# A hybrid RWKV-7 block on one core: other rules for the planner's buffers, four column tiles at the beginning, and a smaller margin

## The chip, the cores and the metric

The kernel runs on one core of a Trainium2 chip. The metric is the device time of one execution in microseconds (us); lower is better. An engine in this text is one of TensorE (PE in the profile; PEld is its weight load), VectorE (DVE), ScalarE (ACT), GpSimd (POOL) and SyncE (SP), which issues the transfers.

## The reference

One layer works on a residual stream x of 1024 positions by 1024 channels, all in float32. Cut to what matters:

```python
h = rms_norm(x, norm_mix)
p = h @ W_in        # columns: r,k,v (512 each) | decay 64 | a 64 | gate 160 | conv b,c,x (512 each) | gates a,b (1024 each)
y_a = rwkv7_branch(...)     # S_t = S_{t-1} diag(w_t) + (S_{t-1} a_t) b_t^T + v_t k_t^T;  y_t = S_t r_t, 8 heads of 64
y_b = B * conv3(C * x_c)
x += (sigmoid(gA) * (y_a @ P_A) + sigmoid(gB) * (y_b @ P_B)) @ W_o
x += cross_attention(rms_norm(x), rms_norm(mem))   # 4 heads of 256, 256 memory tokens: K, V = mem @ w_kv
x += relu(rms_norm(x) @ W_up) ** 2 @ W_down        # 4096 wide
return rms_norm(x)
```

## The kernel before

Channels lie on the partitions and positions in the free dimension, in two blocks of 512 positions (block 0 and 1). A product of the full precision is made in three: each operand is held as a high part in a short float format and the remainder as a low part, and high by high, high by low and low by high are summed in a PSUM bank. So one column tile (128 output channels) over one block is 8 k-tiles of 3 matmuls of 512 columns: 24.

A weight goes through four stages. SP loads it raw (tag `wr`, two buffers), ScalarE makes the high part (`wh`), VectorE subtracts it from the raw one to make the low part (`wl`), TensorE multiplies. `w_loads` (L428) starts load i when the weights before i - 2 are split, and `w_splits` (L515) lets only a few split weights wait for TensorE.

**The order of the work** is not found by the chip. A planner (`Scheduler`, L46 to L243) runs while the program is built: every part of the kernel is a generator that yields the time or condition at which its next step makes sense; `run` takes the streams on the side in turn when they are ready and else the main stream, and every instruction is written to its engine's queue in the order in which it is recorded. The planner's clock is the estimated end of TensorE's queue. `cost` estimates an instruction, `need(t)` is the estimated end of the writes to t plus 0.7 us, `pace(engine)` the end of an engine's queue less 0.3 us. All instructions come from one helper line (L256 in the profile), so groups in the profile are told apart by the tiles. An engine executes its queue in order: where TensorE's next matmul waits, everything behind it waits.

PSUM has 8 banks, in tags: `g` three (projections; `psg` in the profile), `s` two (`pss`), `c` two (`psc`), `y` one (`psy`). Which buffer a new tile of a tag gets is decided by the framework underneath when the program is built. `slot` (L296) is the planner's model of that choice: of the buffers in use, it takes the one whose estimated end is earliest, and counts the new tile as writable from then.

**The beginning.** x arrives in eight row pieces, four for each block. `x_stage(b)` (L1026) transposes them on TensorE in two halves of channels, into banks of `s` and `c`, scales them by the norm's gain, and splits them into high and low (tiles `H`). `gemm` with pair=2 (L826) starts the projection with two column tiles at once: block 0 for both, then block 1 for both; then one column tile after another. `constants` (L707) transposes the small parameter vectors and derives constants on GpSimd.

**The RWKV part** is cut into 8 windows (4 pairs of heads by 2 blocks). `wkv_prepare` (L1274) makes a window's operands; its small matrix products go through the two banks of tag `s` (norms, the four products of `evac_products`, two groups of transposes, bonus, values, and more in `wkv_invert` and `wkv_out`: 13 tiles in each window). They are made as side streams while the projection's large products run. `take_s` and `give_s` count the banks of `s` in use, and a product is recorded when its inputs are `need` + `LATE` old, where `LATE` is 0.7 (L1258).

**The end of the projections.** While the last windows' chains run, the projection of the gates (2 x 8 column tiles) and the memory's keys (`mem_k`, 8 tiles) and values (`mem_v`, 2 x 4 weights) fill TensorE. `HEAD` (L607) is the number of projection tiles that run before the memory's; the last four (`ga` 4 to 7) stand between them: keys 0 to 3, gate tile 4, keys 4 to 7, gate tile 5, first half of the values, gate tile 6, second half, gate tile 7. A weight of the keys or values has half as many product columns as a gate's (`light`).

Then follow the merge of the two branches, the output projection, the attention and the MLP.

Of the kernel before, what the change touches and what calls it, by code (L numbers as in the profile page):

```python
# [41 lines left out]
class Scheduler:  # L42
# [4 lines left out]
    def __init__(self, nc):  # L47
        self.nc = nc
        self.free = {"PE": 0.0, "DVE": 0.0, "ACT": 0.0, "POOL": 0.0, "SP": 0.0, "DMA": 0.0, "LD": 0.0}
        self.writes, self.reads, self.base, self.end = {}, {}, {}, {}  # L50
        self.side = []
        self.cold = 10
        self.mode = (128, 128)
        self.port = {"DVE": [], "POOL": []}
# [13 lines left out]
    def cost(self, eng, meth, aps):  # L68
# [3 lines left out]
        if eng == "ACT":  # L72
            return (0.05 if psum else 0.093) + (0.093 if len(aps) > 2 else 0.0) + n / 1200 + (0.1 if part and n > 64 else 0.0)
        if eng == "DVE":
# [4 lines left out]
            if part:  # L79
                return (0.2 if meth == "scalar_tensor_tensor" else 0.17) + (0.08 if 4 < n <= 64 else 0.0) + n * 0.00104  # L80
            if meth in ("tensor_scalar", "tensor_copy") and not psum:
                return 0.12 + n * 0.00068
# [75 lines left out]
    def note(self, eng, meth, outs, ins):  # L158
# [25 lines left out]
        for a in outs:  # L184
            k, r = self.key(a), self.region(a)
            self.writes[k] = [x for x in self.writes.get(k, ()) if x[1] > old and x[0] != r] + [(r, end, lat, eng)]
            self.end[k] = max(self.end.get(k, 0.0), end)

# [73 lines left out]
def tile_hybrid_block(  # L262
# [31 lines left out]
    slots = {}  # L294

    def slot(tag, t):  # L296
# [113 lines left out]
    def w_raw(i):  # L410
        n = 2 if i in quads else 1
        more = i >= first_quad and (i - first_quad) % 2 if i in quads else i > first_quad and i % 4 > 1
# [15 lines left out]
    def w_loads():  # L428
        for i in range(2, len(wlist)):
# [85 lines left out]
    def w_splits():  # L515
        for i in range(2, len(wlist)):
# [20 lines left out]
            yield lambda: ws["made"] < ws["closed"] + (4 if i < 4 else 2 if i < first_quad else 3)  # L537
# [69 lines left out]
    HEAD = len(PROJ) - 4  # L607
    wcols = [w_cols(win, job_off(k, i), n=32 if (k, i) == ("gd", 1) else P) for k, i in PROJ]
    wlist += wcols[:HEAD]
    for q in range(2):  # L610
        i = len(wlist)
        wlist += [w_cols(w_kv[0], n * P) for n in range(4 * q, 4 * q + 4)]
        light.update(range(i, len(wlist)))
        wlist.append(wcols[HEAD + q])
    for n in range(2):
        i = len(wlist)
        wlist += [w_wide(w_kv[0], kq * 256, D + n * 512) for kq in range(4)]
        light.update(range(i, len(wlist)))
        wlist += wcols[HEAD + 2 + n:HEAD + 3 + n]
# [27 lines left out]
    for i in range(2):  # L647
        w_load_half(i, SP, 1)
    for i in range(4, 8):
# [57 lines left out]
    def constants():  # L707
        yield until(("h", 0, 3))
        yield need(vrow) + 6.0
        vps = ps("g", [P, P])  # L710
# [4 lines left out]
        yield until(("r1", 0))  # L715
# [110 lines left out]
    def gemm(jobs, xh, xl, evac, key=None, scale=None, pair=1):  # L826

        def finish(t, b, o):
            if scale is not None:
                yield until((scale, b))  # L830
            yield room
            evac(t, b, o)

        group = pair
        while jobs:
            now, jobs = jobs[:group], jobs[group:]
            ws_ = []
            for t in now:
                yield from w_take(ws_)
            for b in range(NB):  # L840
                os_ = [ps(t, [P, TB]) for t in (("g", "y") if group == 2 and b else ("g", "g"))[:group]]
                yield need(*os_)
                for k in range(KD):
                    if key is not None:
                        yield until((key, b, k))
                    for (wh, wl), o in zip(ws_, os_):
                        if wl is None:
                            yield need(wh, xl[k][b])
                            mm(o[:], wh[:, k, :], xh[k][b], k == 0, False)
                            yield  # L850
                            mm(o[:], wh[:, k, :], xl[k][b], False, k == KD - 1)
                            yield
                            continue
                        yield need(wl[:, k], xl[k][b])
                        yield from mm3y(o[:], wh[:, k, :], wl[:, k, :], xh[k][b], xl[k][b], k == 0, k == KD - 1)
                if b == NB - 1:
                    for _ in now:
                        w_close()
                for t, o in zip(now, os_):
                    yield from finish(t, b, o)  # L860
            group, key = 1, None
# [151 lines left out]
    def x_scale(b, xs, ss):  # L1013
        cs = slice(0 if b else TB, D)
        junk = sb("P", [P, D]) if b else None
        for i in range(4):
            ACT.activation(junk[:] if b else xs[i][:, cs], xs[i][:, cs], AF.Square, accum_out=ss[:, 4 + i:5 + i])
# [5 lines left out]
        yield from over_partitions(r, Rt[:, b], "g", 4.0 * b)  # L1023
        done.add(("r1", b))

    def x_stage(b, tags):  # L1026
# [3 lines left out]
        if b:  # L1030
            yield until(("h", 0, KD - 1))
        else:
            w_first()
        for h in range(2):
            o = [ps(t, [P, TB]) for t in tags[h]]
            for i in range(4):
                yield need(xs[i][:, h * TB:(h + 1) * TB], *o)
# [82 lines left out]
    def lora_side(name, parts, b, dst, fin):  # L1120
        yield until(("x", 1))
        for j in range(4):
# [11 lines left out]
            fin(z, o2, j)  # L1134
            dma(dst[cs, blk(b)], z, (name, j, b))
# [122 lines left out]
    LATE = 0.7  # L1258
# [6 lines left out]
    def give_s():  # L1265
# [8 lines left out]
    def wkv_prepare(w):  # L1274
# [67 lines left out]
        give_s()  # L1342
# [9 lines left out]
        def evac_products(o, q, h):  # L1352
# [10 lines left out]
            give_s()  # L1363
# [18 lines left out]
        for q in range(2):  # L1382
# [5 lines left out]
            give_s()  # L1388
            ACT.activation(BKt[:, 4 * q:4 * q + 4].rearrange("p c h k -> p c (h k)"), o[:], AF.Copy)
        w["BKt"] = BKt  # L1390
        yield until(("val", j, b))

    def bonus_and_values(w, rk_, vs_, ta_, tm_):
# [20 lines left out]
        give_s()  # L1414
# [15 lines left out]
        give_s()  # L1430
# [14 lines left out]
    def wkv_invert(w):  # L1445
# [46 lines left out]
        give_s()  # L1492
# [10 lines left out]
        give_s()  # L1503

    def wkv_chain(ws):
# [20 lines left out]
        def finish(c):  # L1526
# [3 lines left out]
            if c % 2:  # L1530
                for i, w in enumerate(ws):
                    ACT.activation(flat(w)[:, (c - 1) * C:(c + 1) * C],
                                   Y[c // 2][:, i].rearrange("p a n -> p (a n)"), AF.Copy)

        for c in range(NCH):
# [38 lines left out]
            for q in range(2):  # L1574
# [6 lines left out]
                for h, H, i, w in PART[q]:  # L1581
# [3 lines left out]
                    else:  # L1585
                        DVE.tensor_scalar(new, o2[q][H, 2, i % 2], pc, None, op0=ALU.mult)
            if last:
# [649 lines left out]
```

## Time and profile before

| | us |
|---|---|
| median of 3 runs (lowest, highest) | 1776.28 (1775.63, 1779.83) |
| the profiled execution, its span | 1777.75, 1776.0 |
| TensorE busy | 1726.2 (97%) |
| VectorE, ScalarE, GpSimd busy | 1079.9, 693.2, 520.4 |
| mean granted clock of TensorE | 0.989 |

A row of the page's list of groups or of a timeline names line, engine, operation, output <- inputs, and the shape; in a timeline the start and the length stand ahead, and in brackets how long the engine was idle before it and what released it. A row of the table by stages has the stretch, its length, the busy time of each engine with its instructions, TensorE's granted clock (1.00 is full), the share of the DMA engines' time, and GB/s.

### The profile page before, as it was taken

How to read it: one execution, taken by the hardware profiler on the slowest of the kernel's cores; microseconds unless marked ns; L12 is line 12 of the kernel's file. 1: busy time of each engine (PE TensorE's matmuls, PEld its weight loads, DVE VectorE, ACT ScalarE, POOL GpSimd, SP SyncE). 2: the span in 40 equal slices, each digit the busy share in tenths (PEclk: the TensorE clock that was granted, in tenths of full speed). 3: DMA queues.
4: the chain of work that ended last, by engine and by line, in shares of the span. 5: the costliest groups of instructions: out<-in, count | busy, mean ns of one | idle time of the engine just before them, and what ended most of it. 6: DMA issues, size and time to landing. Idle time of an engine off the chain costs nothing. (4 is left out here: it accounts for less than half of the span.)

```text
span 1776.0 us, 26498 instructions
## 1 busy us (share of the span) xinstructions
PE 1726.2 (97%) x9818; PEld 1421.6 (80%) x9818; DVE 1079.9 (61%) x1700; ACT 693.2 (39%) x1256; POOL 520.4 (29%) x879
## 2 busy tenths in 40 slices
PE   7999999989999999999999999999999999999998
PEld 5787778778778787788888888878888888888887
DVE  4577684556763545565557665596776775555543
ACT  6624221332313563322323434454444453534532
POOL 3136658218286003001313335343323310000000
PEclk9999999999999998999999999999999999999999
DMA  6733533314543428645645667345454489655441
GB/s 215 252 120 99 154 87 86 85 40 133 158 113 117 120 84 273 213 143 202 225 148 166 204 208 253 101 136 179 148 184 149 137 272 351 247 190 190 154 131 48
DMA packets 299007, 289.18 MB, mean 163 GB/s; under 512 B 40488, under 2 KB 217758, under 8 KB 298878
## 3 DMA queue, kind: packets, MB, share of 16 engines
q1 hardware_dynamic: 297806, 286.97, 50.2%
q8 instruction: 77, 1.26, 0.3%
q10 hardware_dynamic: 1072, 0.53, 0.1%
q14 instruction: 52, 0.43, 0.1%
HBM read 193.06 MB, written 94.37 MB: 162 GB/s over the span
## 5 line engine op out<-in xcount | busy, mean ns | idle before, releaser
L256 PE MATMUL psg<-H,wh 128*128 128x512 f32 x1808 | 582.6, 401 | 4.9 <-ACT wh L256 3.5
L256 PEld LDWEIGHTS psg<-H,wh 128*128 128x128 f32 x1808 | 342.1, 191 | 77.4 <-ACT wh L256 4.4
L256 PE MATMUL psg<-P,wh 128*128 128x512 f32 (+1 forms) x1240 | 371.6, 380 | 0.8 <-DVE P L256 0.8
L256 PE MATMUL psg<-H,wl 128*128 128x512 f32 x888 | 354.7, 399 | 0.1
L256 PEld LDWEIGHTS psg<-P,wh 128*128 128x128 f32 x1240 | 228.3, 188 | 44.0 <-DVE P L256 1.2
L256 ACT ACTIVATE wh<-wr 128x1024 fp32r<-128x1024 f32 (+2 forms) x180 | 137.0, 787 | 296.0 <-PE psg L256 200.7
L256 PE MATMUL psg<-P,wl 128*128 128x512 f32 (+1 forms) x620 | 235.5, 380 | 0.0
L256 DVE TENSOR_TENSOR wl<-wr,wh 128x1024 fp32r<-128x1024 f32 (+2 forms) x171 | 166.7, 994 | 60.6 <-ACT wh L256 57.9
L256 PEld LDWEIGHTS psg<-H,wl 128*128 128x128 f32 x888 | 169.8, 191 | 35.9 <-DVE wl L256 0.9
L256 ACT ACTIVATE P<-P 128x512 fp32r<-128x512 f32 (+2 forms) x258 | 153.6, 630 | 81.5 <-DVE P L256 49.9
L256 DVE TENSOR_TENSOR P<-P,P 128x512 fp32r<-128x512 f32 (+2 forms) x221 | 155.8, 740 | 20.7 <-ACT P L256 19.2
L256 POOL TENSOR_TENSOR sm<-sm,mhalf 128x8 f32<-128x8 f32 (+3 forms) x19 | 23.3, 1232 | 464.8 <-DVE sm L256 464.8
L256 PEld LDWEIGHTS psg<-P,wl 128*128 128x128 f32 x620 | 116.6, 188 | 21.4
L256 POOL TENSOR_TENSOR ex<-ex,P 128x60 f32<-128x60 f32 (+24 forms) x248 | 95.9, 387 | 37.2 <-DMA P<-dn 21.3
L256 PE MATMUL pss<-P,wh 128*128 128x512 f32 x304 | 94.5, 390 | 1.6 <-DVE P L256 1.6
L256 POOL TENSOR_TENSOR ex<-ex 128x60 f32<-128x60 f32 (+24 forms) x248 | 90.0, 363 | 19.4
L256 DVE TENSOR_TENSOR P<-psg,P 128x512 f32<-128x512 f32 x44 | 30.3, 688 | 82.6 <-PE psg L256 68.8
L256 DVE TENSOR_TENSOR st<-psg,P 128x512 f32<-128x512 f32 x40 | 27.6, 691 | 75.6 <-PE psg L256 70.5
L256 PEld LDWEIGHTS pss<-P,wh 128*128 128x128 f32 x304 | 57.1, 188 | 14.8 <-DVE P L256 2.9
L256 PE MATMUL psc<-P,wh 128*128 128x512 f32 x216 | 66.5, 389 | 0.0
L256 ACT ACTIVATE P<-P,vec 128x512 f32<-128x512 f32 (+2 forms) x57 | 40.5, 711 | 65.6 <-DVE P L256 54.8
L256 DVE TENSOR_SCALAR P<-psc,sm 64x64 f32<-64x64 f32 x120 | 32.3, 290 | 53.8 <-ACT P L256 53.7
(684 smaller groups left out, 2772.5 us busy)
## 6 DMA issues: line engine op xcount, KB each, us to landing
P<-d_t SPq DMA_DIRECT2D x56, 512.0 KB
wr<-in_w_in_dram SPq DMA_DIRECT2D x40, 512.0 KB
d_t<-P SPq DMA_DIRECT2D x64, 256.0 KB
d_x<-P SPq DMA_DIRECT2D x48, 256.0 KB
P<-d_x SPq DMA_DIRECT2D x24, 512.0 KB
d_t<-st SPq DMA_DIRECT2D x48, 256.0 KB
d_tg<-st SPq DMA_DIRECT2D x32, 256.0 KB
wr<-in_w_kv_dram SPq DMA_DIRECT2D x16, 512.0 KB
```

The source lines that it names most:

```text
L256: return fn(*args, **kw)
```

## The change

The instructions are the same on every engine to within a few; what changes is their order up to the merge. In its parts:

- **The model of the buffers.** The planner counts instructions and keeps, for each tile, the number of its last use. `slot` takes the buffer with the earliest last use, and of those first one that was handed back by a call of `free` (`give_s(o)` does that now with the bank it gives back).
- **Costs.** An activation on less than 128 partitions costs 0.1 us more whatever its length, a scan has its own cost.
- **The beginning.** `gemm_first` does the first four column tiles: 0 and 1 over block 0, 2 and 3 over block 0, then 0 and 1, and 2 and 3 over block 1. The raw weights 2 and 3 are loaded by SP ahead of the second four pieces of x. The transposes of block 1 wait for the parameter vectors ("vec"), which are handed over with 2.0 us instead of 6.0 and in a bank of `s`.
- **The margin.** `LATE` is 0.3.
- **The end of the projections.** Two gate tiles are left (6 and 7): keys 0 to 3, tile 6, keys 4 to 7 and the first half of the values, tile 7, the second half of the values.

```diff
     def slot(tag, t):
         q = slots.setdefault(tag, [])
         if len(q) == BUFS[tag]:
-            old = min(q, key=lambda u: sch.end.get(u, 0.0))
+            old = min([u for u in q if u in used_up] or q, key=lambda u: sch.last.get(u, sch.count + 1))
...
+    def free(*tiles):
+        used_up.update(sch.key(t) for t in tiles)
...
-            yield lambda: ws["made"] < ws["closed"] + (4 if i < 4 else 2 if i < first_quad else 3)
+            yield lambda: ws["made"] < ws["closed"] + (4 if i < 6 else 2 if i < first_quad else 3)
...
-    HEAD = len(PROJ) - 4
+    HEAD = len(PROJ) - 2
...
     for i in range(2):
         w_load_half(i, SP, 1)
+    for i in range(2, 4):
+        w_load(i, w_raw(i))
     for i in range(4, 8):
         x_load(i)
...
     def constants():
-        yield until(("h", 0, 3))
-        yield need(vrow) + 6.0
-        vps = ps("g", [P, P])
+        yield until(("r1", 0))
+        yield need(vrow) + 2.0
+        vps = ps("s", [P, P])
...
+    def gemm_first(jobs, xh, xl, evac, key, scale):
...
+        for b in range(NB):
+            for q in range(2):
+                now = jobs[2 * q:2 * q + 2]
...
+                os_ = [ps(t, [P, TB]) for t in ("gg", "gy")[q]]
+                yield need(*os_)
+                for k in range(KD):
+                    yield until((key, b, k))
+                    for (wh, wl), o in zip(ws_[2 * q:2 * q + 2], os_):
+                        yield need(wl[:, k], xl[k][b])
+                        yield from mm3y(o[:], wh[:, k, :], wl[:, k, :], xh[k][b], xl[k][b], k == 0, k == KD - 1)
...
-    LATE = 0.7
+    LATE = 0.3
...
-    def give_s():
+    def give_s(o):
+        free(o)
         open_s["n"] -= 1
...
-        yield from gemm(PROJ[:HEAD], hh, hl, proj_evac, key="h", scale="r1", pair=2)
-        for q in range(4):
-            for n in range(4 * q, 4 * q + 4) if q < 2 else ():
+        yield from gemm_first(PROJ[:4], hh, hl, proj_evac, "h", "r1")
+        yield from gemm(PROJ[4:HEAD], hh, hl, proj_evac, scale="r1")
+        for q in range(2):
+            for n in range(4 * q, 4 * q + 4):
                 yield from mem_k(n)
-            if q > 1:
-                yield from mem_v(q - 2)
+            if q:
+                yield from mem_v(0)
             yield from gemm(PROJ[HEAD + q:HEAD + q + 1], hh, hl, proj_evac, scale="r1")
+        yield from mem_v(1)
+        drop(4)
```

What this does to the order is shown at three places. The first is TensorE in the beginning (`psg` and `psy` are projection banks, `P` here a piece of x, `ident` the identity of the transposes; the number behind a name tells one tile from another). Before, where the eighth k-tile of block 0 ends and block 1 begins for the same two column tiles:

```order
L256 MATMUL psg_195<-H_175,wh_186 128x512
L256 MATMUL psg_195<-H_167,wl_187 128x512
L256 MATMUL psg_196<-H_167,wh_188 128x512
L256 MATMUL psg_196<-H_175,wh_188 128x512
L256 MATMUL psg_196<-H_167,wl_189 128x512
L256 MATMUL psg_384<-ident,sm_363 128x128 x4
L256 MATMUL pss_445<-ident,P_98 128x128
L256 MATMUL pss_446<-ident,P_98 128x128
L256 MATMUL psc_447<-ident,P_98 128x128
L256 MATMUL psc_448<-ident,P_98 128x128
L256 MATMUL psg_440<-H_160,wh_186 128x512
```

Of the change, the same place:

```order
L261 MATMUL psg_200<-H_171,wh_192 128x512
L261 MATMUL psg_200<-H_179,wh_192 128x512
L261 MATMUL psg_200<-H_171,wl_193 128x512
L261 MATMUL psg_358<-H_164,wh+_57_253 128x512
L261 MATMUL psg_358<-H_172,wh+_57_253 128x512
L261 MATMUL psg_358<-H_164,wl+_58_254 128x512
L261 MATMUL pss_363<-ident,sm_353 128x128 x4
L261 MATMUL psy_359<-H_164,wh+_59_264 128x512
```

After the last k-tile of block 0 the change goes on with the third and fourth weight (`wh+`) over block 0; the first transposes of block 1 (`P_102` there) stand 15 rows further on, among these products.

The second is VectorE in the preparation of one window, at the products of `evac_products` (`pss` with `msk` or `sm` as the second input) and the bonus. Before:

```order
L256 TENSOR_TENSOR P_1880<-pss_2108,sm_2093 64x256
L256 TENSOR_TENSOR P_2119<-P_1880,P_2119 128x512
L256 TENSOR_TENSOR wl_2123<-wr_1903,wh_2122 128x1024
L256 TENSOR_TENSOR P_1966<-pss_2108,msk 64x512
L256 SCALAR_TENSOR_TENSOR st_2144<-sh_2125,vec,st_2144 128x512
L256 TENSOR_TENSOR P_1872<-pss_2108,msk 64x256
L256 TENSOR_TENSOR P_1880<-pss_2109,sm_2093 64x256
L256 TENSOR_TENSOR P_1967<-pss_2109,msk 64x512
L256 TENSOR_TENSOR P_1873<-pss_2156,P_1873 128x512
```

Of the change:

```order
L261 TENSOR_TENSOR P_1828<-pss_2102,sm_2090 64x256
L261 TENSOR_TENSOR P_1964<-pss_2102,msk 64x512
L261 TENSOR_TENSOR P_2116<-P_1828,P_2116 128x512
L261 TENSOR_TENSOR P_1820<-pss_2102,msk 64x256
L261 TENSOR_TENSOR sh_2130<-psg_2055,P_188 128x512
L261 TENSOR_TENSOR P_1828<-pss_2103,sm_2090 64x256
L261 TENSOR_TENSOR wl_2128<-wr_1901,wh_2127 128x1024
L261 TENSOR_TENSOR P_1965<-pss_2103,msk 64x512
```

The three readers of the first product's bank stand closer together, and the weight's subtraction and the gate step have moved behind them.

The third is SP in the beginning. Before, the four pieces of x for block 1 follow the two halves of the first weights:

```order
L256 DMA P_82<-in_x_dram 128x512
L256 DMA wr_88<-in_w_in_dram 128x4x128
L256 DMA wr_90<-in_w_in_dram 128x4x128
L256 DMA P_98<-in_x_dram 128x1024
L256 DMA P_100<-in_x_dram 128x1024
```

Of the change:

```order
L261 DMA wr_88<-in_w_in_dram 128x4x128
L261 DMA wr_90<-in_w_in_dram 128x4x128
L261 DMA wr+_8_98<-in_w_in_dram 128x8x128
L261 DMA wr+_9_100<-in_w_in_dram 128x8x128
L261 DMA P_102<-in_x_dram 128x1024
L261 DMA P_104<-in_x_dram 128x1024
```

Two whole weights now stand ahead of the pieces of x.

More of the change, by code (lines that the diff above doesn't have):

```diff
@@ L49, in __init__ @@
         self.free = {"PE": 0.0, "DVE": 0.0, "ACT": 0.0, "POOL": 0.0, "SP": 0.0, "DMA": 0.0, "LD": 0.0}
-        self.writes, self.reads, self.base, self.end = {}, {}, {}, {}
+        self.writes, self.reads, self.base, self.end, self.last = {}, {}, {}, {}, {}
         self.side = []
         self.cold = 10
+        self.count = 0
         self.mode = (128, 128)
@@ L72, in cost @@
         if eng == "ACT":
-            return (0.05 if psum else 0.093) + (0.093 if len(aps) > 2 else 0.0) + n / 1200 + (0.1 if part and n > 64 else 0.0)
+            return (0.05 if psum else 0.093) + (0.093 if len(aps) > 2 else 0.0) + n / 1200 + (0.1 if part else 0.0)
         if eng == "DVE":
@@ L187, in note @@
             self.end[k] = max(self.end.get(k, 0.0), end)
+        self.count += 1
+        self.last.update((self.key(a), self.count) for a in ins + outs)
     def shared(self, eng, st, end):
@@ L294, in tile_hybrid_block @@
     slots = {}
+    used_up = set()
     def slot(tag, t):
@@ L428, in w_loads @@
     def w_loads():
-        for i in range(2, len(wlist)):
+        for i in range(4, len(wlist)):
             if i < first_quad:
@@ L612, in tile_hybrid_block @@
         wlist += [w_cols(w_kv[0], n * P) for n in range(4 * q, 4 * q + 4)]
+        if q:
+            wlist += [w_wide(w_kv[0], kq * 256, D) for kq in range(4)]
         light.update(range(i, len(wlist)))
         wlist.append(wcols[HEAD + q])
[L615 to L619, printed above, removed]
+    i = len(wlist)
+    wlist += [w_wide(w_kv[0], kq * 256, D + 512) for kq in range(4)]
+    light.update(range(i, len(wlist)))
     wlist += [w_pair(w_proj_b[0], w_proj_a[0], n * P) for n in range(KD)]
@@ L714, in constants @@
         DVE.tensor_copy(vec[:], vps[:])
-        yield until(("r1", 0))
+        free(vps)
+        done.add("vec")
         cv["omu"] = derived("omu", "mu", -1.0, 1.0)
@@ L845, in gemm @@
                         yield until((key, b, k))
[L846 to L855, printed above, removed]
-                if b == NB - 1:
[L857 to L861, printed above, removed]
+                    if wl is None:
+                        yield need(wh, xl[k][b])
+                        mm(o[:], wh[:, k, :], xh[k][b], k == 0, False)
+                        yield
+                        mm(o[:], wh[:, k, :], xl[k][b], False, k == KD - 1)
+                        yield
+                        continue
+                    yield need(wl[:, k], xl[k][b])
+                    yield from mm3y(o[:], wh[:, k, :], wl[:, k, :], xh[k][b], xl[k][b], k == 0, k == KD - 1)
+                if b == NB - 1:
+                    w_close()
+                if scale is not None:
+                    yield until((scale, b))
+                yield room
+                evac(t, b, o)
+            key = None
     PRODUCTS = ((1, "g", 0, 0), (2, "c", 0, 1), (6, "g", 1, 0), (5, "s", 1, 1), (7, "g", 2, 0), (3, "s", 2, 1),
@@ L1030, in x_stage @@
         if b:
-            yield until(("h", 0, KD - 1))
+            yield until("vec")
         else:
@@ L1036, in x_stage @@
             for i in range(4):
-                yield need(xs[i][:, h * TB:(h + 1) * TB], *o)
+                yield need(xs[i][:, h * TB:(h + 1) * TB], *o) if not (b and h and i) else None
                 for k in range(4):
@@ L1134, in lora_side @@
             fin(z, o2, j)
+            free(o2)
             dma(dst[cs, blk(b)], z, (name, j, b))
@@ L1533, in finish @@
                                    Y[c // 2][:, i].rearrange("p a n -> p (a n)"), AF.Copy)
+                free(Y[c // 2])
         for c in range(NCH):
@@ L1586, in wkv_chain @@
                         DVE.tensor_scalar(new, o2[q][H, 2, i % 2], pc, None, op0=ALU.mult)
+            free(*o2)
             if last:
```

63 lines of the change are left out of this document (39 added, 24 removed).

## The prediction

> **What bounds the kernel now.** I read the page first, then TensorE's waits, then a table by stage.
>
> ```profile
> PE 1726.2 (97%) x9818; PEld 1421.6 (80%) x9818; DVE 1079.9 (61%) x1700; ACT 693.2 (39%) x1256; POOL 520.4 (29%) x879
> PE pss L256 <- DVE P L256: 12.8, 13, 2.6
> PE pss L256 <- issue: 4.5, 3, 2.4
> core 0: us, PE busy (x) PEld busy (x) DVE busy (x) ACT busy (x) POOL busy (x), PEclk, DMA share, GB/s
> 23.00:62.00 39.00, 33.74 (x151) 26.57 (x152) 24.02 (x41) 28.35 (x50) 10.58 (x38) 0.91 0.64 208
> 62.00:700.00 638.00, 614.97 (x4720) 503.02 (x4719) 385.76 (x740) 221.20 (x490) 279.47 (x670) 0.98 0.41 122
> 700.00:735.00 35.00, 33.49 (x147) 26.99 (x146) 19.08 (x24) 13.80 (x24) 7.95 (x6) 1.00 0.77 245
> 735.00:1762.00 1027.00, 1019.94 (x4682) 845.93 (x4681) 637.96 (x877) 413.55 (x658) 214.33 (x147) 1.00 0.55 182
> ```
>
> TensorE is the bound: 97% busy, and it gets exactly the same products after the change. So only its idle time and its clock can move. The table says where these are: 5.3 us idle in the beginning (39.00 - 33.74), 23.0 in the long stretch to 700, 1.5 in the 35 us after it, 7.1 in the thousand after that. From the attention on (735) the instructions of every engine stand in the old order, so I carry that part over at no difference; only its start shifts. Everything is decided before 735, where the idle time comes to 29.8 us, and the granted clock, below 1.00 in the first two rows alone, adds more. The waits say who makes TensorE idle: mostly VectorE, and on the two tiles "pss", the banks of the preparation's small products.
>
> **The clock.** The long waits for those banks, and the 3.41 us stretches round some of them:
>
> ```profile
> 218.64 0.71 PE L256 MATMUL pss<-P,bdo 128*128 128x512 f32 x2 [1.75 <-DVE P L256]
> 234.11 0.79 PE L256 MATMUL pss<-P,P 32*32 32x32 f32 x32 [2.36 <-issue]
> 368.06 0.70 PE L256 MATMUL pss<-P,bdo 128*128 128x512 f32 x2 [2.56 <-DVE P L256]
> 384.17 1.01 PE L256 MATMUL pss<-P,P 64*128 64x128 f32 x13 [1.51 <-DVE P L256]
> 466.57 0.78 PE L256 MATMUL pss<-P,P 32*32 32x32 f32 x32 [1.43 <-issue]
> 494.46 0.84 PE L256 MATMUL pss<-P,P 64*128 64x128 f32 x8 [1.58 <-DVE P L256]
> 232.09:235.50 3.41, 1.39 (x35) 1.29 (x36) 3.29 (x7) 0.56 (x2) 0.00 (x0) 1.00 0.89 243
> 235.50:238.92 3.42, 3.42 (x10) 2.57 (x9) 2.63 (x5) 1.34 (x3) 2.34 (x4) 0.50 0.43 115
> 368.62:372.03 3.41, 3.41 (x21) 2.39 (x21) 1.04 (x2) 0.00 (x0) 0.00 (x0) 0.50 0.20 77
> 385.69:389.11 3.42, 3.42 (x16) 2.65 (x13) 2.21 (x7) 1.13 (x4) 0.00 (x0) 0.50 0.00 0
> 467.61:471.02 3.41, 3.41 (x9) 2.64 (x8) 2.06 (x5) 2.26 (x4) 2.31 (x6) 0.50 0.00 0
> 494.91:498.33 3.42, 3.42 (x18) 2.71 (x15) 2.71 (x5) 0.00 (x0) 2.95 (x7) 0.50 0.32 125
> ```
>
> The six waits sum to 11.19 us. Behind five of them stands one stretch of 3.41 us at a granted clock of 0.50, in which TensorE does the work of 1.7 us: five times 1.7 is 8.5 us more. The wait at 218.64 has no such stretch behind it. So a wait of 1.4 to 2.6 us costs its length and usually 1.7 us on top; whether it does hangs on how it lies to the borders of the stretches. The Trainium skill's page "TensorE: Matmul & The Clock Gate" (section on the HAM clock gate) gives the same window, 3413 ns and free-running, but has the clock fall after at least one idle window of about 3.4 us. This trace disagrees on the size: the stretch 232.09 to 235.50 has 1.39 us of work in it, and the next one is at 0.50 all the same.
>
> **Part 1, the beginning.** Before, the first projection does two column tiles over block 0 and then must have block 1, whose transposes, vectors and normed halves are made just then:
>
> ```profile
> 23.27 0.30 PE L256 MATMUL pss<-ident,P 128*128 128x128 f32 x1 [0.74 <-issue]
> 24.57 0.30 PE L256 MATMUL pss<-ident,P 128*128 128x128 f32 x1 [1.00 <-DVE P L256]
> 30.75 0.60 PE L256 MATMUL psg<-ident,sm 128*128 128x128 f32 x4
> 33.59 0.30 PE L256 MATMUL psc<-ident,P 128*128 128x128 f32 x1 [1.01 <-DVE bdo L256]
> 35.59 0.45 PE L256 MATMUL psc<-ident,P 128*128 128x128 f32 x1 [1.69 <-DVE H L256]
> 50.96 0.39 PE L256 MATMUL psg<-H,wh+_62_342 128*128 128x512 f32 x1
> 1177.57 2.72 PE pss L256 x12
> 6.92 2.72 SPq L256 DMA_DIRECT2D wr<-in_w_in_dram  x2
> 9.69 1.94 SPq L256 DMA_DIRECT2D P<-in_x_dram  x4
> ```
>
> Two tiles times two blocks times 24 products are 96 products of 512 columns, done at 50.96. One such product takes 2.72/12 = 0.227 us at full clock, so without more waits 144 are done at 50.96 + 48 x 0.227 = 61.9. In the change, two more tiles over block 0 stand where block 1 was waited for. Block 0 of the first two tiles ends at 30.75 now, with the first sixteen transposes of block 1 (four of them take some 0.43 us there, so 1.7 together) and the two waits of 0.74 and 1.00 us for them inside; in the change these come later, so it ends near 30.75 - 1.7 - 1.7 = 27.3. Then come the third and fourth tile over block 0 (48 x 0.227 = 10.9) with block 1's first transposes among them (1.7), to 39.9, and the first two tiles over block 1 (10.9) with the second transposes (1.7) and one wait of about 1.2 us for the halves that ScalarE and VectorE make from these, to 53.7. The gain is 61.9 - 53.7 = 8.2 us: the waits, the work around them, and the half clock that follows them now (the granted clock is 0.91 in the first row of the table). I take 6.5, because the walk takes no second wait and one full clock throughout, and a stretch at half clock would cost 1.7. The bounds: at least the two waits at 33.59 and 35.59, 2.7, in round numbers 3; at most the walk with that wait gone, 9. What speaks against it: two more weights of 512 KB go out on SP's queue ahead of block 1's four pieces of x (the two weight halves took 2.72 us to issue, the four pieces 1.94). At the 208 GB/s of the table's first row a megabyte makes x 5 us later. That is hidden as long as block 1's transposes come after 27, since the pieces were all issued by 11.6.
>
> **Part 2, the banks and the order of VectorE.** For 218.64 the rows of VectorE show what the wait is made of:
>
> ```profile
> 213.88 0.41 DVE L256 TENSOR_TENSOR P<-pss,sm 64x256 f32<-64x256 f32 x1
> 215.32 1.22 DVE L256 TENSOR_TENSOR wl<-wr,wh 128x1024 fp32r<-128x1024 f32 x1
> 216.57 0.69 DVE L256 TENSOR_TENSOR P<-pss,msk 64x512 f32<-64x512 f32 x1
> 217.29 0.75 DVE L256 SCALAR_TENSOR_TENSOR st<-sh,vec,st 128x512 f32<-128x512 f32 x1
> 218.07 0.42 DVE L256 TENSOR_TENSOR P<-pss,msk 64x256 f32<-64x256 f32 x1
> ```
>
> TensorE's next small product takes the bank that the last of these frees, at 218.49. Between its first and last reader, 4.6 us, stand a weight's subtraction (1.22), a gate step (0.75) and another product of 512 columns (0.69 us, as its neighbours). The planner held another bank for the next one, so it saw no need to hurry. In the change the three readers stand with one step of 0.69 between them: 0.41 + 0.69 + 0.69 + 0.42 = 2.2 us, against 12 products of 512 columns on TensorE in that time, 2.7 us. So the wait goes. At 234 it is alike: two scans (1.27 us together) stand between the readers now and behind them in the change, and TensorE has 15 large products instead of 6 in between, 3.4 us for 1.5. The other four I take over from these two, since they fall on the same tiles (where the profile puts "issue" as the releaser, as at 234.11, nothing later than VectorE's reader ended before). That is 11.2 + 8.5 = 19.7 us won, if no such wait comes up elsewhere; the bounds are 8 (the two places I followed, 1.75 + 2.36 + 1.7, and one more like them) and 19.7.
>
> Against this stands the margin. Of the preparation's products, 13 on these banks in each of 8 windows, 104 in all, each is handed to TensorE 0.4 us closer to the planned end of its inputs (0.3 instead of 0.7, beside the 0.7 that every `need` has). Behind a product that comes too early the whole projection queues, as TensorE takes its work in order. Rows for what that costs are the waits where the margin was spent already: thirteen of them on "pss" sum to 12.8 us, the four long ones above among them make 7.4, so the other nine are of some 0.6 us. A product that was just in time can now be late by at most the 0.4 taken away. I take one in six, 17, late by all of it: 7 us lost. The bounds are 0 (all are covered by the 1.0 that remains) and 40 x 0.4 = 16. The smaller margin gives nothing back on TensorE by itself, because a projection stood in the gap; it makes the windows' chains ready earlier, and of those none is waited for before 735.
>
> **Part 3, the end of the projections.** Two gate tiles instead of four are left between the light weights of the memory's keys and values, so eight light ones run in a row. The costs that bear on it:
>
> ```profile
> 688.36 0.38 SPq L256 DMA_DIRECT2D wr<-in_w_in_dram  x1
> 695.50 1.34 ACT L256 ACTIVATE wh<-wr 128x256 fp32r<-128x256 f32 x4 [3.20 <-DMA wr<-in_w_in_dram]
> 695.97 0.95 PE L256 MATMUL psg<-H,wh 128*128 128x512 f32 x2 [2.68 <-ACT wh L256]
> 690.00:700.00 10.00, 7.25 (x25) 5.08 (x24) 5.98 (x11) 5.61 (x13) 3.17 (x3) 0.83 0.98 355
> ```
>
> A light weight keeps TensorE for 12 products of 512 columns, 2.72 us, and its 512 KB must come in that time; where DMA is full (share 0.98) one load took 695.50 - 688.36 = 7.1 us, and TensorE stood 2.68 us. With two loads under way that is one each 3.6 us, 0.8 more than 2.72. Against it, the two gate tiles that go forward leave their own loads out of this stretch, and TensorE's time for them (48 products, 10.9 us each) stays the same elsewhere. I take +2: the wait of 2.68 at 695.97 moves rather than goes, and 4 of the 8 lose a part of 0.8. The bounds are -1 (that wait goes in part) and 8 x 0.8 = +6.4, and 1.7 for a stretch at half clock: +8.
>
> The rest I cost at nothing. The transpose of the parameter vectors that is handed over earlier is one of 0.11 us, and the constants made from it run on POOL, 29% busy. The changed costs only move rows. A stretch at half clock of another kind stays, since the products ahead of it, two columns wide, stand in the same place in the change:
>
> ```profile
> 667.83 2.34 PE L256 MATMUL pss<-bd,P 128*128 128x2 f32 x16
> 669.01:672.42 3.41, 3.41 (x12) 2.93 (x13) 0.51 (x2) 0.00 (x0) 3.41 (x3) 0.50 0.43 163
> ```
>
> **The sum.** -6.5 - 19.7 + 7 + 2 = -17.2 us. The profiled execution took 1777.75 us (span 1776.0), 1.5 above the median of 1776.28; the sum is a difference, and set on the median it gives 1759.
>
> **The rivals.** *The waits move.* The thirteen waits on "pss" are a matter of which reader stands last, and with every row shifted they come up at other places of the same length; the change is then worth the beginning and the tail alone: 1776.3 - 6.5 + 2 = 1771.8. For it speaks that the planner's costs are means, and that I followed only two of six places; against it that both cures come from the rule for the bank, which holds everywhere. *The margin costs what the banks give.* With 40 late products, 16 us, and three of them grown long enough for a stretch at half clock, 5: -6.5 - 19.7 + 21 + 2 = -3.2, 1773. For it: the products' inputs come from VectorE, which in the rows above runs up to 1.2 us behind one step; against: VectorE has 252 of 638 us free in that stage. *The clock does not follow the waits.* If the stretches at 0.50 come on their own account, or small waits that straddle a border take over, the waits go and the 8.5 us stay: 1767.6. Against it speak five of six long waits with such a stretch behind them. By the clock rule of the Trainium skill's page "TensorE: Matmul & The Clock Gate" (section on the HAM clock gate) it would go like this, since none of these waits is a whole window; the trace leaves that little chance. *Slower: the light weights starve.* If DMA is full through the whole end, each of 12 light weights (the last four of the keys too) comes in (7.1 + 2)/2 = 4.6 us, with 2 for its two halves' conversion before the buffer is free: 1.8 more than 2.72, 12 x 1.8 = 22 us, and five stretches at half clock, 8.5. That puts the whole at 1776.3 - 19.2 + 30.5 = 1788. It decides once each of the 12 loses over 19.2/12 = 1.6 us, a period of 4.3. For it: 355 GB/s at a share of 0.98 is as much as the trace shows; against: the row for 700 to 735 has a share of 0.77, and TensorE waits 1.5 us in it.
>
> **How the numbers follow.** A difference under 0.3% (5.3 us) is what a measurement of this kernel can't tell from none. The forecast gets 0.50, with 1750 to 1766 as its own range; the clock staying 0.17; the waits moving 0.14; the margin 0.11; the starving loads 0.08. The range reaches from 1749 (all bounds on the good side but one: -9 - 19.7 + 2 - 1) to 1774, which leaves out the last rival and a part of the margin's. Faster by over 0.3% is below 1771: the forecast and the clock rival whole, 0.67, about half of the two between 1771.8 and 1773, 0.12: 0.79. Within: the other half, 0.13. Slower: 0.08.
>
> **What would show it.** Part 1: the first product of the fifth column tile, or the 144th large one, near 54 and no wait over 1.3 us between 27 and 54. Part 2: no "pss" wait for VectorE over 1 us between 62 and 660, the sum of 12.8 + 4.5 down below 9, and no stretch at 0.50 there but those after the products of two columns. The margin: more waits of under 0.5 us on "pss" and "psc", whose number tells the term. Part 3: the time of the values' products between the last window's inputs and the attention, and waits for "ACT wh". Wrong would be: waits over 1.4 us on "pss" as many as before, or a stage from 690 to 735 that is more than 8 us longer.

## The result and the profile after

The change takes 1753.18 us (median of six runs, 1748.14 to 1754.73) against 1775.95 for the kernel before: a ratio of 0.9864, 95% interval 0.9844 to 0.9883, so 24 us less by the ratio (20.8 to 27.7 by the interval) and 22.8 by the medians. The forecast was 1759, 17.2 less. One of the five executions of the kernel with the old costs below, the traced one, ran at a granted clock of 0.556 throughout (2844.75 us) and is left out of that kernel's figures.

Of the page of the changed kernel the busy time of the engines and the granted clock; of its waits on TensorE the three that matter:

```profile
PE 1714.2 (98%) x9818; PEld 1414.2 (81%) x9818; DVE 1081.8 (62%) x1697; ACT 692.8 (40%) x1253; POOL 527.5 (30%) x879
PEclk9999999999999998999999999999999999999999
PE psg L261 <- DVE wl L261: 5.0, 5, 1.9
PE pss L261 <- DVE P L261: 3.7, 4, 2.1
PE psg L261 <- ACT wh L261: 2.0, 2, 1.8
```

TensorE is 12 us less busy with the same products, and the waits on the small products' banks for VectorE fell from 12.8 us to 3.7; the "issue" waits there are gone from the list. The largest group of waits is now the low part of a weight; 3.6 of its 5.0 us stand at the end of the projections.

The table by stage (stretch, its length, busy time of each engine, granted clock, DMA share, GB/s), cut at 62 and at 560, where the last inverse products begin; first before, then the change:

```profile
14.00:62.00 48.00, 42.27 (x188) 33.19 (x188) 29.17 (x49) 33.17 (x61) 12.74 (x41) 0.93 0.59 199
62.00:560.00 498.00, 482.61 (x3322) 391.80 (x3321) 315.55 (x556) 148.64 (x279) 264.32 (x644) 0.98 0.40 116
560.00:735.00 175.00, 165.85 (x1545) 138.22 (x1544) 89.29 (x207) 86.36 (x235) 23.10 (x32) 0.97 0.52 164
```

```profile
14.00:62.00 48.00, 47.73 (x234) 39.13 (x234) 32.05 (x50) 33.70 (x60) 15.91 (x45) 1.00 0.65 225
62.00:560.00 498.00, 492.00 (x3456) 401.30 (x3455) 322.19 (x571) 158.87 (x301) 270.50 (x659) 0.99 0.41 119
560.00:735.00 175.00, 165.53 (x1483) 136.89 (x1482) 95.16 (x208) 80.39 (x218) 19.16 (x13) 0.97 0.56 177
1044.15 61.05 PE psg L261 x268
```

TensorE's idle time in the three stages was 5.7, 15.4 and 9.2 us and is 0.3, 6.0 and 9.5. The last row, of the chain of waits, is the first long run of products in the attention: it began at 1069.62 and begins at 1044.15, 25.5 earlier. So the whole difference lies ahead of it, as forecast, and by its idle time and clock the end of the projections gave nothing.

The beginning, and the place in VectorE's timeline that the prediction followed (the preparation of the third window, now at 201 us), with TensorE's bonus product behind it:

```profile
52.76 0.73 PE L261 MATMUL psg<-H,wh+_57_253 128*128 128x512 f32 x2 [0.27 <-ACT P L261]
201.07 0.69 DVE L261 TENSOR_TENSOR P<-pss,msk 64x512 f32<-64x512 f32 x1
201.78 0.69 DVE L261 TENSOR_TENSOR P<-P,P 128x512 fp32r<-128x512 f32 x1
202.49 0.42 DVE L261 TENSOR_TENSOR P<-pss,msk 64x256 f32<-64x256 f32 x1
203.63 0.63 PE L261 MATMUL pss<-P,bdo 128*128 128x512 f32 x2
```

The 144 products of the beginning are done by 52.76, where 53.7 was worked out, and 61.9 for the kernel before. In the table the beginning has 5.4 us less idle time, and its clock of 1.00 for 0.93 makes (1.00 - 0.93) x 48 = 3.4 us more, together 8.8. The bank's last reader ends at 202.91, the bonus product takes it at 203.63 without a wait; it waited 1.75 us.

One long wait on such a bank is left between 62 and 560, and two stretches at half clock have no wait ahead. The last three products (L256) and the last stretch are of the kernel before:

```profile
460.39 1.22 DVE L261 TENSOR_TENSOR wl<-wr,wh 128x1024 fp32r<-128x1024 f32 x1
462.59 0.41 DVE L261 TENSOR_TENSOR P<-pss,sm 64x256 f32<-64x256 f32 x1
463.01 1.12 DVE L261 TENSOR_TENSOR P<-pss,msk 64x512 f32<-64x512 f32 x2
464.28 0.71 PE L261 MATMUL pss<-P,bdo 128*128 128x512 f32 x2 [2.12 <-DVE P L261]
380.56 1.95 PE L261 MATMUL pss<-bd,P 128*128 128x2 f32 x16
382.93 0.95 PE L261 MATMUL pss<-bd,P 128*128 128x2 f32 x8
385.56 1.70 PE L261 MATMUL pss<-bd,P 128*128 128x2 f32 x8
461.80:465.20 3.40, 1.28 (x6) 0.81 (x5) 3.34 (x6) 0.00 (x1) 2.99 (x6) 1.00 0.66 155
465.70:469.10 3.40, 3.40 (x9) 2.65 (x9) 3.31 (x8) 2.19 (x4) 2.75 (x11) 0.50 0.26 98
383.60:387.00 3.40, 3.40 (x15) 3.02 (x14) 1.10 (x3) 0.00 (x0) 3.17 (x7) 0.53 0.41 154
387.00:390.40 3.40, 3.40 (x12) 2.81 (x12) 0.84 (x3) 0.00 (x0) 3.32 (x4) 0.50 0.00 0
405.21 1.95 PE L256 MATMUL pss<-bd,P 128*128 128x2 f32 x16 [0.21 <-ACT P L256]
408.03 0.95 PE L256 MATMUL pss<-bd,P 128*128 128x2 f32 x8
410.08 0.95 PE L256 MATMUL pss<-bd,P 128*128 128x2 f32 x8
408.60:412.00 3.40, 3.40 (x22) 3.01 (x22) 1.63 (x5) 0.72 (x1) 3.32 (x6) 1.00 0.00 0
```

At 464 VectorE does the readers in one piece, as wanted, but began them late, behind a weight's subtraction and a step of the bonus. TensorE works 1.28 of the 3.4 us round this wait, and behind it the granted clock is 0.50 for 3.4 us. From 383.6 on there are two more such stretches (0.53 and 0.50) with no wait ahead: what stands ahead are products of two columns, for which the page counts TensorE busy. That these products are the cause isn't shown: sixteen, eight and eight of the same kind in the kernel before, from 405.21 on, are followed by a clock of 1.00.

At the end of the projections the light weights wait, with their load as the releaser of ScalarE in front:

```profile
663.09 0.50 PE L261 MATMUL psg<-wh,P 128*128 128x512 f32 x1 [1.80 <-ACT wh L261]
670.64 0.79 PE L261 MATMUL psg<-wl,P 128*128 128x512 f32 x1 [1.86 <-DVE wl L261]
673.99 0.80 PE L261 MATMUL psg<-wl,P 128*128 128x512 f32 x1 [1.71 <-DVE wl L261]
667.59 1.15 ACT L261 ACTIVATE wh<-wr 128x512 fp32r<-128x512 f32 x2 [3.77 <-DMA wr<-in_w_kv_dram]
```

### The profile page after: what moved, and what is told of

Same layout as the page of the kernel before. It is cut to its first block, busy times and chain, and to the rows that moved or that the text cites. A ratio compares the mean times of both kernels' runs of the same rounds, so it can differ in the third digit from the quotient of the medians.

```text
span 1751.4 us, 26520 instructions
## 1 busy us (share of the span) xinstructions
PE 1714.2 (98%) x9818; PEld 1414.2 (81%) x9818; DVE 1081.8 (62%) x1697; ACT 692.8 (40%) x1253; POOL 527.5 (30%) x879
## 5 line engine op out<-in xcount | busy, mean ns | idle before, releaser
L261 DVE TENSOR_TENSOR wl<-wr,wh 128x1024 fp32r<-128x1024 f32 (+2 forms) x168 | 162.5, 986 | 61.5 <-ACT wh L261 60.8
L261 DVE TENSOR_TENSOR P<-P,P 128x512 fp32r<-128x512 f32 (+2 forms) x221 | 161.9, 769 | 21.4 <-ACT P L261 20.1
L261 POOL TENSOR_TENSOR ex<-ex 128x60 f32<-128x60 f32 (+24 forms) x248 | 89.0, 359 | 19.4
L261 DVE TENSOR_TENSOR P<-psg,P 128x512 f32<-128x512 f32 x44 | 30.3, 689 | 79.9 <-PE psg L261 66.4
L261 ACT ACTIVATE P<-psc,sm 64x64 f32<-64x64 f32 (+1 forms) x128 | 39.1, 329 | 51.7 <-DVE P L261 29.5
```

The costliest lines, as they stand in the source:

```text
L261: return fn(*args, **kw)
```

## The experiments

Times are medians; a ratio is against the runs of the kernel before on the same chip (1776.6, 1777.6 and 1780.4 us in the three groups of runs), with its interval.

### The margin back at 0.7

```diff
-    LATE = 0.3
+    LATE = 0.7
```

> The change with the margin LATE back at 0.7; all else as changed (1753.2 us, 22.8 less than before). Theory A (the prediction's term: the smaller margin costs 7 us): 1746, fewer short waits than the change on the small products' banks. Theory B (the 1.0 us that remains covers the products; read from the trace of after, whose waits on these banks for VectorE sum to 3.7 us against 12.8): 1751 to 1755, no difference to tell. Theory C (the margin itself is what pays, by handing the products over at better places): 1758 or more.

Measured: 1743.37 us, ratio 0.9810 (0.9792 to 0.9827). This is 9.8 us less than the change, A's direction and a little more than its size. The two stages, the waits on the banks and the longest wait of TensorE:

```profile
62.00:560.00 498.00, 495.30 (x3485) 404.70 (x3484) 326.06 (x568) 158.01 (x297) 270.77 (x655) 1.00 0.42 121
560.00:735.00 175.00, 163.13 (x1487) 137.13 (x1486) 98.05 (x218) 84.74 (x226) 20.25 (x18) 0.98 0.54 178
PE pss L261 <- DVE P L261: 1.6, 3, 0.7
589.58 1.12 PE L261 MATMUL psc<-s,P 64*64 64x64 f32 x16 [4.85 <-ACT s L261]
```

Idle time in the middle falls from 6.0 to 2.7 us, and the granted clock rises. But the number of waits on the banks is three instead of four: there is no crowd of late products to take away. What went in the middle is the one wait at 464 and two of the three stretches at half clock. From 560 on this kernel idles more than the change (11.9 us for 9.5), 4.85 of it in one wait at the chain of the last windows, and is faster all the same. From 14 to 735 the two differ by only 0.9 us of idle time (15.7 and 14.8); the mean clock of the runs makes some 5 of the 9.8 (below), and the rest isn't located.

### The old rule for the banks

```diff
-            old = min([u for u in q if u in used_up] or q, key=lambda u: sch.last.get(u, sch.count + 1))
+            old = min(q, key=lambda u: sch.end.get(u, 0.0))
```

> The change with the planner's old choice of the reused buffer (earliest estimated end); all else as changed. Theory A (the rule for the banks brought the middle's 19.7 us): 1765 to 1773, waits on the small products' banks of 1.4 us and more come back, four to six of them, and stretches at half clock behind them. Rival B (the waits went because every row was shifted, not by the rule): 1750 to 1757, waits as in the change.

Measured: 1780.54 us, ratio 1.0019 (1.0007 to 1.0030), so all of the gain and a little more is gone. A's waits came back, four of them of over 1.4 us between 62 and 560; its size was too small, since the time lies 7.5 above its range. The middle, and one of the waits that came back:

```profile
62.00:560.00 498.00, 480.15 (x3295) 389.94 (x3294) 317.27 (x555) 151.79 (x286) 261.50 (x632) 0.98 0.40 115
144.86 0.41 DVE L261 TENSOR_TENSOR P<-pss,sm 64x256 f32<-64x256 f32 x1
145.95 0.69 DVE L261 TENSOR_TENSOR P<-pss,msk 64x512 f32<-64x512 f32 x1
149.52 0.40 DVE L261 TENSOR_TENSOR P<-pss,msk 64x256 f32<-64x256 f32 x1
150.07 0.85 PE L261 MATMUL pss<-P,bdo 128*128 128x512 f32 x2 [1.89 <-DVE P L261]
```

Idle time in the middle is 17.9 us. The three readers of the bank take 5.1 us from the first to the third, with one other step between the first and the second and four between the second and the third, and TensorE waits for the third. `slot` serves every tag, so this run and the next change the planner's model of all buffers; that it is the banks of the small products that count is read from the waits that come and go.

### The rule for the banks alone

The kernel before, with the instruction count, the last uses, `free` and `give_s(o)` of the change and nothing else.

```diff
-            old = min(q, key=lambda u: sch.end.get(u, 0.0))
+            old = min([u for u in q if u in used_up] or q, key=lambda u: sch.last.get(u, sch.count + 1))
```

> The kernel before with the rule for the banks alone (the model of the buffers with the calls that hand back; old beginning, margin 0.7, old costs, old end). Theory A (the rule pays by itself what it cost to undo it, 27.4 us, or the 19.7 us of the prediction's six waits): 1749 to 1758, the six waits of 1.4 to 2.6 us on the small products' banks gone or down to one. Rival B (it pays only with the other parts in place): 1768 or more.

Measured: 1758.74 us, ratio 0.9891 (0.9874 to 0.9909), so 19.4 us less (16.2 to 22.4), 0.7 above the upper end of A's range and far from B's. The middle, the end and the waits:

```profile
62.00:560.00 498.00, 495.41 (x3495) 404.85 (x3494) 321.12 (x568) 157.81 (x297) 268.45 (x661) 1.00 0.42 122
560.00:735.00 175.00, 164.34 (x1461) 139.78 (x1460) 94.94 (x208) 81.81 (x223) 20.30 (x13) 0.92 0.53 170
PE pss L259 <- DVE P L259: 6.4, 8, 3.3
```

The six waits between 62 and 560 are gone: 2.6 us idle there for 15.4, clock 1.00 for 0.98. The longest that is left (3.3) stands at 567, at the last window's inverse, which TensorE reaches earlier than its data; behind it the clock falls, and the stage from 560 on has 0.92.

### The new beginning alone

The kernel before, with `gemm_first`, the loads and the handing over of the vectors as in the change, and nothing else.

```diff
-        yield from gemm(PROJ[:HEAD], hh, hl, proj_evac, key="h", scale="r1", pair=2)
+        yield from gemm_first(PROJ[:4], hh, hl, proj_evac, "h", "r1")
+        yield from gemm(PROJ[4:HEAD], hh, hl, proj_evac, scale="r1")
```

> The kernel before with the new beginning alone (four column tiles over block 0, weights 2 and 3 ahead of x, vectors earlier; old rule for the banks, margin 0.7, old costs, old end). Theory A (it pays the 8.3 us by which the first bonus product comes earlier in the change): 1766 to 1770, no wait over 1 us between 23 and 54. Rival B (the lead is lost to other waits further on, since the old rule leaves them): 1773 to 1779.

Measured: 1775.96 us, ratio 0.9995 (0.9983 to 1.0007): nothing, as rival B had it. Its beginning, its waits on the banks and its two stages behind:

```profile
42.14 0.30 PE L256 MATMUL psc<-ident,P 128*128 128x128 f32 x1 [1.55 <-DVE H L256]
55.73 0.73 PE L256 MATMUL psg<-H,wh+_57_253 128*128 128x512 f32 x2 [1.75 <-ACT P L256]
PE pss L256 <- DVE P L256: 19.0, 19, 3.2
62.00:560.00 498.00, 478.96 (x3341) 387.87 (x3340) 319.12 (x558) 150.48 (x284) 264.07 (x648) 0.99 0.40 116
560.00:735.00 175.00, 166.08 (x1507) 139.97 (x1506) 86.99 (x207) 86.19 (x234) 21.62 (x24) 0.95 0.51 162
```

With the old rule the beginning itself has two waits that the change has not (1.55 and 1.75 us, of which 0.27 is left there), so 144 products are done at 55.7, not 52.8: a lead of 6. The waits on the banks then sum to 19.0 us, where they were 12.8, and the middle has 19.0 us of idle time where the kernel before had 15.4. That accounts for 3.6 of the 6. From 560 on the clock is 0.95 for 0.97, which is 3.5 us of 175, while in the middle it is a little higher (0.99 for 0.98); so the lead is spent by 735, but how the rest divides between the two is not resolved at this rounding.

### The old end

```diff
-    HEAD = len(PROJ) - 2
+    HEAD = len(PROJ) - 4
```

with the lists of weights and the loop at the end as they were.

> The change with four gate tiles left to the end, as before. Theory A (the row of eight light weights costs the 2.5 us by which the lead shrinks between 514 us and the attention): 1750 to 1751.5, the three waits of 1.7 to 1.9 us on light weights go. Rival B (the old end has the same waits at its gate tiles): 1753 to 1756.

Measured: 1754.80 us, ratio 0.9873 (0.9855 to 0.9892). Against the change's 0.9864 (0.9844 to 0.9883) that is no difference: the time lies in B's range, and A's 2.5 us are not there. B's reason is not what the trace shows, though. Of the light weights' three waits one is left (1.64 us), and two others stand at the last window's inverse and chain:

```profile
566.66 0.31 PE L261 MATMUL pss<-P,P 32*32 32x32 f32 x2 [2.68 <-DVE P L261]
576.91 1.12 PE L261 MATMUL psc<-s,P 64*64 64x64 f32 x16 [2.54 <-ACT s L261]
```

### The old costs

```diff
-            return (0.05 if psum else 0.093) + (0.093 if len(aps) > 2 else 0.0) + n / 1200 + (0.1 if part else 0.0)
+            return (0.05 if psum else 0.093) + (0.093 if len(aps) > 2 else 0.0) + n / 1200 + (0.1 if part and n > 64 else 0.0)
...
-            if meth == "tensor_tensor_scan":
-                return 0.07 + n * 0.0023
```

> The change with the planner's old costs for scans and small activations. Theory A (they only move rows): 1750 to 1756. Rival B (the scan's cost is what moved the scans behind the bank's readers): 1758 or more, with waits over 1.4 us on the small products' banks.

Measured: 1746.60 us (median of four), ratio 0.9826 (0.9809 to 0.9843), 6.6 less than the change. The changed costs brought nothing, they rather took; A's band begins 3.4 us higher, and B's lies higher still, so neither theory held. What made it faster stays open.

### The margin at 0.7 with the old costs

> The change with the margin at 0.7 and the planner's old costs for scans and small activations. Theory A (both undone parts add: 9.8 and 6.0 us): 1736 to 1740. Theory B (the costs only deal another order): 1742 to 1752.

Measured: 1741.78 us, ratio 0.9801 (0.9783 to 0.9819). The parts don't add: 9.8 and 6.6 would make 1736.8. The time lies between the two theories' ranges, 0.2 below B's. With the margin at 0.7 the costs make 1.6 us, within the scatter. It is nominally the fastest kernel of the study together with the margin of 0.5 below, faster than before and than the change.

```profile
62.00:560.00 498.00, 496.03 (x3499) 405.47 (x3498) 328.06 (x576) 162.21 (x305) 270.44 (x659) 1.00 0.43 123
```

TensorE has 2.0 us of idle time left in that stage.

### Other margins

```diff
-    LATE = 0.3
+    LATE = 1.0
```

> The change with the margin at 1.0 instead of 0.3 (0.7 gave 1743.4, 9.8 less than the change). Theory A (less margin makes late products, so more margin costs nothing): 1738 to 1746. Theory B (each value of the margin only deals another order, and the times scatter by some 10 us): outside these bounds, 1748 or more among them. Theory C (more margin holds the chains back until they are waited for): 1748 or more with a wait of several us near the last window's inverse, about 590 us.

> The change with the margin at 0.0 instead of 0.3. Theory A (each step of the margin taken away makes more products late): 1757 to 1768, more waits on the small products' banks than the 3.7 us of the change. Theory B (the margin's values only deal orders that scatter): 1741 to 1754.

> The change with the margin at 0.5. Theory A (the cost falls with the margin, 1753.2 at 0.3 and 1743.4 at 0.7): 1746 to 1751. Theory B (scatter): anywhere from 1741 to 1755, outside A's bounds as likely as in them.

> The change with the margin at 0.75, a step of 0.05 from 0.7 (1743.4) that means nothing to the products but writes another order, from the row where the first window's products begin. Theory A (the margin's size sets the time): 1742 to 1745. Theory B (every new order scatters): more than 3 us away from 1743.4.

Measured, in the order of the margin (the change is the row of 0.3), with the mean granted clock of the runs and the product of mean time and mean clock, an estimate of the time that would be left at full clock:

| margin | median us | ratio, interval | clock | time x clock |
|---|---|---|---|---|
| 0.0 | 1749.87 | 0.9844 (0.9824 to 0.9864) | 0.994 | 1739 |
| 0.3 | 1753.18 | 0.9864 (0.9844 to 0.9883) | 0.9935 | 1741 |
| 0.5 | 1743.15 | 0.9800 (0.9780 to 0.9821) | 0.996 | 1736 |
| 0.7 | 1743.37 | 0.9810 (0.9792 to 0.9827) | 0.9965 | 1737 |
| 0.75 | 1744.85 | 0.9808 (0.9789 to 0.9827) | 0.997 | 1740 |
| 1.0 | 1747.40 | 0.9835 (0.9815 to 0.9855) | 0.994 | 1738 |

A margin of 0.0 takes 1750, where a cost of late products asked for 1757 or more, and 0.5 takes as little as 0.7, below the range of a cost that falls with the margin: the cost doesn't grow with what is taken away. Nor do the times scatter by 10 us with each new order, since 0.75 lies 1.5 from 0.7. The margin of 1.0 lies between the ranges of its theories, and no wait of several us stands near the last inverse, as theory C of that run had it. At full clock the six lie within 5 us. Of the 9.8 us between 0.3 and 0.7, the clock makes (0.9965 - 0.9935) x 1750 = 5.

### The rule for the banks alone, margin 0.3

The same as the rule alone above, with the smaller margin.

> The kernel before with the rule for the banks alone and the margin at 0.3 (with 0.7: 1758.7). Theory A (the smaller margin costs about as much as in the change, where it was 9.8): 1764 to 1772. Theory B (scatter, or no cost): 1752 to 1762.

Measured: 1758.96 us, ratio 0.9893 (0.9875 to 0.9911), against 0.9891 with 0.7. The margin costs nothing here that the intervals of 3 us would show (B).

## Why the prediction was right, point by point

- **What bounds the kernel.** Right. The gain came ahead of the attention, from idle time (30.3 us between 14 and 735 before, 15.7 after) and from the clock (0.989 in the profiled execution before, 0.993 after: 7 us of 1750). Together that is 21.6 of the 24.6 us by which the profiled spans differ; the remaining 3 aren't located.
- **The beginning, -6.5.** As a walk it was right: 52.8 where it had 53.7, and the wait of 1.2 us in it is 0.27. Idle time and clock of that stage make 8.8, above the -6.5 that was taken and just inside the bound of 9. As a term it was wrong in standing by itself. Alone the beginning gives nothing (0.9995). With the old rule for the banks there are two waits in it of 1.55 and 1.75 us, and the waits behind it take the lead back.
- **The banks, -19.7.** The rule alone measures -19.4. The waits that were named went, at the two places that were followed and at the four that were taken over: 15.4 us of idle time became 2.6 between 62 and 560. The makeup was not quite as worked out: the half clock behind those waits went too, but the waits and a half clock from 567 on took a part of it back; of the 19.4 us, time at full clock makes 17 (1759 to 1742) and the clock the rest. Undoing the rule in the change costs 27.4, so it is worth more there than alone. The likely reason is that it keeps the new beginning's gain as well.
- **The margin, +7.** The sign was right, the mechanism wrong. The step "I take one in six, 17, late by all of it" is not what happened: the change has four waits on these banks for VectorE, the same kernel at 0.7 has three, and on the other base the margin costs nothing. The "0.4 us closer" was not right for all 13 either: ahead of the four products the kernel has `2 * LATE`, so these moved by 0.8. What the change has in the middle and 0.7 has not is one wait of 2.12 us, the half clock behind it and one more stretch of half clock. Whether 0.3 brings that with it, or this one order does, the runs don't settle. That the loss is 9.8 where 7 was put is luck.
- **The end, +2.** Not to be told from zero: with the old end 1754.80 for 1753.18. Its waits are there (1.80, 1.86 and 1.71 us, with ScalarE waiting 3.77 for a load), but the kernel with the old end has others (2.68 and 2.54 us at the last windows).
- **The rest at nothing.** Wrong for the costs, which "only move rows": undoing them gave 6.6 us in the change, 1.6 at a margin of 0.7. A term of a few us either way belonged to the range.
- **The rivals.** "The waits move" is what happened to the new beginning alone, and not to the banks. "The margin costs what the banks give": no. "The light weights starve": they wait, by a quarter of what that rival had. "The clock does not follow the waits": half right. The clock fell behind the wait at 464, and with the rule alone the waits and the half clock in the middle went together. But the stretches from 383.6 on have no wait ahead, so long waits are not all that it goes by.
- **What would show it.** The 144th product near 54 and no wait over 1.3 between 27 and 54: both so (52.8, and 0.27). No "pss" wait over 1 us between 62 and 660: there is one for VectorE, at 464. Sum below 9: 3.7. No half clock but behind the two-column products: one stretch behind the wait at 464, and those at the end; and the products of two columns that had one before (at 667.83) are not the ones that have it now (at 380.56), so that kind did not stay in its place. More short waits as the sign of the margin: none, 13 waits on "pss" for VectorE became four, and six on "psc" became seven.

Why the forecast was 6 us short: by stage, idle time and half clock of the traces give -8.8 at the beginning, where -6.5 was put, and +0.3 at the end for +2. In the middle they give -12.8 (9.4 us of idle time, and three stretches at half clock for five, 3.4), where -19.7 + 7 = -12.7 was put. The rest, some 3 us, the stages don't show. The banks' -19.7 was read from rows, and with the margin at 0.7 the middle gives 12.7 + 6.8 = 19.5. But that the whole sum came so near is in part luck, since two errors of opposite sign partly cancel. Without the margin and the costs the sum would have been -6.5 - 19.7 + 2 = -24.2; the kernel with 0.7 and the old costs is 35 us below the one before (ratio 0.9801). And margin and costs together take back 11.4, where 7 and nothing were put. The parts measured one at a time don't add either: the rule alone gives 19.4 of these 35, the beginning alone nothing, and where the other 15 come from no run separates.

## What to carry to other kernels

When a planner decides the order, the rule by which it guesses which buffer is reused next is worth a test of its own: here the new rule alone gave 19.4 us, because the readers of the bank that was needed next came earlier. That the new rule is the framework's own was not measured. An earlier start is worth something only when the stages behind it don't wait for something else anyway; measure it with that other wait taken away. And small constants of a planner are set by a sweep on the chip, the step from 0.3 to 0.7 was worth 10 us here, and its size says little about the reason.

## What was not expected of the hardware

The granted clock differs between executions of one and the same program, and the time goes with it. Of the kernel with a margin of 0.0 the five runs took 1743.84 us at a mean clock of 0.997, 1748.35 and 1749.87 at 0.994, 1752.35 at 0.993 and 1753.05 at 0.992: 0.005 of 1748 is 8.7 us, and 9.2 is the spread. So the same order meets more half clock in one execution than in another; with 1.7 us for a stretch, 9 us is about five of them. That a bare median of two orders differs by 5 us need not mean that either has less to wait for; the mean clock has to be read beside it.

The Trainium skill's page "TensorE: Matmul & The Clock Gate" (section on the HAM clock gate) says that the clock's window runs freely and doesn't begin with the kernel. The runs here are in keeping with that, in that the mean clock of one order differs from execution to execution (0.992 to 0.997). They don't agree with a whole idle window of some 3.4 us as what it takes: the wait of 2.12 us at 464, with 1.28 us of work in the 3.4 us round it, was followed by half clock. Nor does a longer wait always bring it. In the kernel with a margin of 0.5 the clock stays at 1.00 behind a wait of 2.90 us:

```profile
661.51 0.50 PE L261 MATMUL psg<-wl,P 128*128 128x512 f32 x1 [2.90 <-DVE wl L261]
661.50:664.90 3.40, 3.10 (x13) 2.26 (x13) 1.99 (x4) 1.68 (x3) 0.00 (x0) 1.00 1.00 374
```

That would fit a window that runs freely, in which the place of a wait counts as well as its length; no run here shows the windows' borders.
